# A two-layer hybrid transformer block on one Trainium2 core: 1/rms rows spread in one pass of 96 rows, modulation rows summed on four column groups, wider h tiles

## The chip, the cores and the metric

One core of a Trainium2 chip runs the whole program. TensorE multiplies matrices into PSUM, VectorE and ScalarE work on vectors, and the DMA queues are driven by SyncE. The metric is the time of one execution on the device in microseconds (us), lower is better, as the median of several runs.

## What is computed

Two layers of a diffusion trunk act on 512 latent and 256 context tokens of width 1024, all in float32. Cut to what matters here:

```python
def rms_norm(x, g):
    y = x * lax.rsqrt(jnp.mean(x * x, axis=-1, keepdims=True) + EPS)
    return y * g

mod_x = silu(c) @ w_mod + b_mod            # 6 x 1024 numbers a layer, for latents; mod_c for context
hx = rms_norm(x, norm1_g) * (1 + sc1x) + sh1x
parts = split(hx @ w_in)                   # q, k, v (and a gate) of four head groups
q = rope_2d(rms_norm(to_heads(q), qnorm_g), rows, cols)      # rms over a head of 64 or 32
out = concat(windowed, differential, retention, neighbourhood attention)
x = x + g1x * (out @ w_out)
h2 = rms_norm(x, norm2_g) * (1 + sc2x) + sh2x
x = x + g2x * (square(relu(h2 @ w_mlp1)) @ w_mlp2)
```

The context tokens go through the same weights in the first layer; in the second one only the latents are carried to the end.

## The kernel before

Activations stand transposed: features on the 128 partitions, tokens along the row, eight tiles of 128 x 768 for a width of 1024. Every large product is split into a rounded part and a rest, each of which TensorE takes in its one-pass float32 type (`F32R`), and is made of three products: `gemm` (L317, L318, L322) runs hi x hi, hi x lo and lo x hi over the feature chunks, first 512 columns, then the remaining 256 or 258. Its moving operand comes from the h tiles (`htile`, names hh, hl, oh, ol) or from the mid tiles of the MLP (mh, ml). `wload` brings weights by DMA (wr) and `split` makes wh on ScalarE (L275) and wl on VectorE (L276).

A norm is done in three steps. The mean of squares is a full float32 product with `gmean`, 32 output columns wide, on blocks of 256 tokens; block j writes the PSUM rows 32j to 32j+31 of one tile (L241 for heads, with two more products L243 where a term is added; L262 for the whole width). `rsqrt` turns the 32, 64 or 96 rows into 1/rms on ScalarE and VectorE. `finish` splits the result into a rounded part and a rest (rr, side by side along the row) and spreads each block over 128 partitions with two products (L257): one for the rounded part, one for the rest. Calls with 768 tokens have three blocks, those with 512 two, those with 256 one; all of the first layer's attention has three, the second layer's has three for keys and two for queries and head outputs.

The modulation of the first layer is computed partly on TensorE (L346, `mod_mm`, four groups of 32 PSUM rows). The remaining 14 blocks of 512 numbers, two of the first layer and all twelve of the second, are worked off by `mods_dve` beside the first layer's MLP: VectorE accumulates over 1024 features into `acc` (L396, L398), partition by partition, for both vectors c and c_ctx; then the 128 partitions have to be summed. For that `acc` is split into `az` tiles and multiplied with a two-column selector (L406, four products of 512 columns), ScalarE copies the two rows out of PSUM (L408), four small transposes (L412) turn them into columns, and `mod_add` (L340) adds the bias.

`weave` lays out the attention: a stream of input projections fills in between the attention units by hand-set cost numbers, and a scheduler orders each engine's instructions from that. Each engine then works its queue in order.

Of the kernel before, what the change touches and what calls it, by code (L numbers as in the profile page):

```python
# [12 lines left out]
OP = mybir.AluOpType  # L13
# [141 lines left out]
def body(ctx: ExitStack, tc, A):  # L155
# [18 lines left out]
    def pst():  # L174
        return pp.tile([128, 512], F32, name=nm("pt"), tag="pt", bufs=PTB)
# [18 lines left out]
    spread = cons.tile([128, 3, 128], F32R, name="spread")  # L194
    with tc.tile_pool(name="sp0", bufs=1) as sp0:
        t = sp0.tile([128, 3, 128], F32, name="spread0")
        V.memset(t, 0.0)
        for j in range(3):
            V.tensor_copy(t[32 * j:32 * j + 32, j].rearrange("p (g c) -> p g c", c=32),
                          ident[32 * j:32 * j + 32, 32 * j:32 * j + 4].unsqueeze(2).to_broadcast([32, 4, 32]))  # L200
        S.activation(spread, t, AF.Copy)
# [24 lines left out]
    sel2 = cons.tile([128, 2, 2], F32, name="sel2")  # L226
    V.memset(sel2, 0.0)
    for v in range(2):
        V.memset(sel2[:, v, v:v + 1], 1.0)
    sel2r = cons.tile([128, 2, 2], F32R, name="sel2r")  # L230
    S.activation(sel2r, sel2, AF.Copy)

    def rstd(ps, sq, n, w, rr, add=None):

        nb = n // 256
        pm = ps[-1][0][0:32 * nb, 0:256]
        for j in range(nb):
            pj = pm[32 * j:32 * j + 32]  # L240
            T.matmul(pj, lhsT=gmean[w], rhs=sq[:, 256 * j:256 * j + 256], start=True, stop=add is None)  # L241
            for i in range(0 if add is None else 2):
                T.matmul(pj[:, 128 * i:128 * i + 128], lhsT=add[:, 8 * j + 4 * i:8 * j + 4 * i + 32], rhs=ident, start=False, stop=(i == 1))  # L243
        finish(pm, ps, sq, rr, add is None)

    def finish(pm, ps, sq, rr, eps=True):

        n = pm.shape[0]
        q, e3 = sq[0:n, 0:256], sq[0:n, 256:512]
        rsqrt([(pm, 0, 256)], q, e3, 256, eps)  # L250
        rr = rr[0:n]
# [177 lines left out]
    def norm_stat(pm, y, s, l, pools=(pst, pst)):  # L429

        ps = [(f()[:, :b], a, b) for f, (a, b) in zip(pools, [(0, l)] if l < 512 else halves(l))]
        finish(pm[0:l // 8, 0:256], ps, zm(), main.tile([128, 768], F32R, name=nm("rr"), tag="zm", bufs=2))
        for p, a, b in ps:
            S.activation(y[:, s + a:s + a + b], p, AF.Copy)
        return y[:, s:s + l]
# [15 lines left out]
    def htile(p):  # L451
        return main.tile([128, 770], F32R, name=nm(p), tag="h", bufs=16)
# [13 lines left out]
    for L in range(DEPTH):  # L466
# [369 lines left out]
        def at_b(u, q, k, v):  # L836
# [4 lines left out]
            for hh in range(2):  # L841
                rows = slice(64 * hh, 64 * hh + 64)
                for n2 in range(nblk // 2):
# [25 lines left out]
                    for i in range(0, len(kts), 2):  # L869
# [7 lines left out]
                        for a in range(2):  # L877
# [6 lines left out]
            lsq = cons.tile([128, 56], F32, name=nm("lsq"), tag="lsq", bufs=1)  # L884
            V.memset(lsq, EPS)
            S.activation(lsq[:, 0:4 * nblk].rearrange("p (n h c) -> p n h c", h=2, c=2),
                         l0[:, 0:nblk].unsqueeze(3).to_broadcast([128, nblk, 2, 2]), AF.Square, scale=EPS ** 0.5)
# [208 lines left out]
        finish(ms[0:nq // 8, 0:256], ps, zm(), main.tile([128, 768], F32R, name=nm("rr"), tag="zm", bufs=2))  # L1096
# [203 lines left out]
```

## Time and profile before

| | us |
|---|---|
| median of 3 runs | 1883.28 (1882.71 to 1885.18) |
| profiled execution | 1887.48 |
| its span, first to last instruction | 1885.7 |
| busy: TensorE / its weight loads / VectorE / ScalarE | 1847.7 / 1520.6 / 1301.7 / 981.6 |

The span falls into the start (up to about 30 us), the first layer's attention (to 525), its output projection, the first layer's MLP (560 to 1095), the norm between the layers, the second layer's attention (1135 to 1505), and the output projection and MLP of the second layer (to 1880). The profile is read from the engines' busy times, then by stage, then by the rows of single instructions. A matrix product's recorded length includes its way through the pipeline, so records overlap; the distance from one start to the next tells what it occupies.

### The profile page before, as it was taken

What the parts mean: (1) busy time and instruction counts of PE and PEld (TensorE: products, weight loads), DVE (VectorE), ACT (ScalarE), POOL (GpSimd) and SP (SyncE); (2) the same over time, 40 slices, a digit from 0 to 9 for tenths busy, and PEclk for the clock granted to TensorE, in tenths of its full rate; (3) what the DMA queues carried; (4) which work ended last, traced back from release to release, by engine and by line L of the source; (5) the groups of instructions that cost most, each with busy time, mean ns of one, the idle gap of its engine ahead of it and who ended that gap; (6) DMA issues with size and microseconds to landing.
All of it is one profiled execution on the core that took longest, in us unless ns stands there. A gap on an engine that the chain in (4) does not pass through costs nothing.

```text
span 1885.7 us, 29731 instructions
## 1 busy us (share of the span) xinstructions
PE 1847.7 (98%) x10899; PEld 1520.6 (81%) x10899; DVE 1301.7 (69%) x3005; ACT 981.6 (52%) x1934; POOL 0.2 (0%) x4
## 2 busy tenths in 40 slices
PE   7998999999999999999999999999999999999999
PEld 3786777778868888888888777888677788989897
DVE  5787877788767847847847367898888664545453
ACT  4677766768563323323324356877677663434241
POOL 0000000000000000000000000000000000000000
PEclk8999999999999999999999999999999999999999
DMA  8324434432323433433422352233243233232222
GB/s 299 100 83 117 126 106 124 148 101 65 123 85 115 145 101 112 150 97 116 152 90 90 112 170 87 79 106 84 78 135 97 75 100 97 91 99 92 96 90 95
DMA packets 110418, 208.69 MB, mean 111 GB/s; under 512 B 14272, under 2 KB 20160, under 8 KB 110272
## 3 DMA queue, kind: packets, MB, share of 16 engines
q1 hardware_dynamic: 110272, 206.78, 34.9%
q8 instruction: 86, 1.41, 0.3%
q14 instruction: 60, 0.49, 0.1%
HBM read 182.09 MB, written 5.24 MB: 99 GB/s over the span
## 4 chain that ended last, share of the span: by engine, by line
PE 83%; ACT 4%; DVE 3%; DMA 1%; issue 1%; DVEq 0%; ACTq 0%
PE mm L317 22%; PE mm L318 22%; PE mm L322 22%; PE ps L701 2%; PE po L707 2%; PE po L709 2%; PE ps L854 1%; PE ps L262 1%; PE pt L873 1%; PE pt L241 1%; PE mm L346 1%; PE pt L257 1%; ACT pth L275 1%; ACT P L756 1%; PE pt L406 1%
## 5 line engine op out<-in xcount | busy, mean ns | idle before, releaser
L275 ACT ACTIVATE wh<-wr 128x512 fp32r<-128x512 f32 (+1 forms) x414 | 253.3, 614 | 592.2 <-PE mm L318 541.1
L317 PE MATMUL mm<-hh,wh 128*128 128x512 f32 (+2 forms) x1680 | 521.2, 329 | 1.0 <-ACT hh L443 0.6
L318 PE MATMUL mm<-hl,wh 128*128 128x512 f32 (+2 forms) x1680 | 518.2, 327 | 0.0
L276 DVE TENSOR_TENSOR wl<-wr,wh 128x512 fp32r<-128x512 f32 (+1 forms) x414 | 275.0, 667 | 203.3 <-ACT wh L275 133.4
L322 PE MATMUL mm<-hh,wl 128*128 128x512 f32 (+2 forms) x1680 | 362.6, 326 | 2.3 <-DVE wl L276 2.3
L317 PEld LDWEIGHTS mm<-hh,wh 128*128 128x128 f32 x1680 | 318.5, 190 | 37.1 <-issue 9.4
L318 PEld LDWEIGHTS mm<-hl,wh 128*128 128x128 f32 x1680 | 318.0, 189 | 30.3 <-issue 5.3
L322 PEld LDWEIGHTS mm<-hh,wl 128*128 128x128 f32 x1680 | 262.7, 189 | 30.5 <-issue 3.1
L317 PE MATMUL mm<-mh,wh 128*128 128x512 f32 (+1 forms) x768 | 264.4, 356 | 0.3 <-DVE mh L1120 0.3
L318 PE MATMUL mm<-ml,wh 128*128 128x512 f32 (+1 forms) x768 | 264.5, 355 | 0.0
L322 PE MATMUL mm<-mh,wl 128*128 128x512 f32 (+1 forms) x768 | 180.7, 355 | 0.0
L317 PEld LDWEIGHTS mm<-mh,wh 128*128 128x128 f32 x768 | 145.0, 189 | 23.1 <-DVE mh L1120 0.9
L318 PEld LDWEIGHTS mm<-ml,wh 128*128 128x128 f32 x768 | 145.1, 189 | 22.2 <-issue 1.6
L398 DVE SCALAR_TENSOR_TENSOR acc<-wm,silp,acc 128x512 f32<-128x512 f32 x196 | 140.8, 747 | 22.3 <-DMA wm<-in_wmod_dram 21.6
L322 PEld LDWEIGHTS mm<-mh,wl 128*128 128x128 f32 x768 | 131.2, 189 | 23.3 <-issue 3.7
L276 DVE TENSOR_TENSOR ptl<-pt,pth 128x512 fp32r<-128x512 f32 (+3 forms) x148 | 92.3, 631 | 30.4 <-ACT pth L275 28.0
L707 PE MATMUL po<-pth,vv 128*128 128x256 f32 (+2 forms) x328 | 105.8, 329 | 3.5 <-ACT pth L275 2.8
L1131 DVE SCALAR_TENSOR_TENSOR x<-mm,modc,x 128x512 f32<-128x512 f32 (+1 forms) x96 | 63.2, 658 | 61.9 <-PE mm L322 61.9
L275 ACT ACTIVATE pth<-pt 128x512 fp32r<-128x512 f32 (+3 forms) x148 | 80.0, 547 | 29.2 <-PE pt L873 17.3
L1115 DVE TENSOR_TENSOR zq<-mm,nacc 128x256 f32<-128x256 f32 (+1 forms) x128 | 61.9, 485 | 45.2 <-PE mm L322 43.1
L707 PEld LDWEIGHTS po<-pth,vv 128*128 128x128 f32 x328 | 62.1, 190 | 26.2 <-ACT pth L275 18.8
L709 PE MATMUL po<-ptl,vv 128*64 128x256 f32 (+2 forms) x256 | 77.6, 315 | 2.5 <-DVE ptl L276 2.3
(251 smaller groups left out, 2684.4 us busy)
## 6 DMA issues: line engine op xcount, KB each, us to landing
wr<-in_w_dram SPq DMA_DIRECT2D x272, 256.0 KB, 2.6
wm<-in_wmod_dram SPq DMA_DIRECT2D x112, 256.0 KB, 2.8
wr<-in_win_dram SPq DMA_DIRECT2D x96, 256.0 KB, 3.1
wr<-in_wmodh_dram SPq DMA_DIRECT2D x48, 256.0 KB, 3.3
st<-sp SPq DMA_DIRECT2D x96, 96.0 KB, 2.2
w<-in_wmod_dram SPq DMA_DIRECT2D x16, 384.0 KB, 7.0
tx<-in_dd_dram SPq DMA_DIRECT2D x8, 512.0 KB, 3.6
zm<-in_dd_dram SPq DMA_DIRECT2D x16, 256.0 KB, 3.0
```

What stands on the lines that cost most here:

```text
L241: T.matmul(pj, lhsT=gmean[w], rhs=sq[:, 256 * j:256 * j + 256], start=True, stop=add is None)
L275: S.activation(hi, src, AF.Copy)
L276: V.tensor_tensor(lo, src, hi.bitcast(F32), op=OP.subtract)
L317: T.matmul(p, lhsT=w[k][0], rhs=act[k][0][:, s:s + l], start=(k == 0), stop=False)
L318: T.matmul(p, lhsT=w[k][0], rhs=act[k][1][:, s:s + l], start=False, stop=False)
L322: T.matmul(p, lhsT=w[k][1], rhs=act[k][0][:, s:s + l], start=False, stop=(k == n - 1))
L398: V.scalar_tensor_tensor(acc[:, v], r, sil[:, k, v:v + 1], acc[:, v], op0=OP.mult, op1=OP.add)
L701: T.matmul(o, lhsT=x, rhs=y, start=(i == 0), stop=(i == 1))
L707: T.matmul(po[:, c0:c0 + l], lhsT=vv[:, hh, t], rhs=ph, start=start, stop=stop)
L709: T.matmul(po[0:64, c0:c0 + l], lhsT=vv[:, hh, t, 0:64], rhs=pl, start=False, stop=False)
L1115: V.tensor_tensor(r[:, s:s + l], p[:, :l], y2[:, s:s + l], op=OP.mult)
L1131: V.scalar_tensor_tensor(xx, p, modc[:, 40 + m, s // 512:s // 512 + 1], xx, op0=OP.mult, op1=OP.add)
```

## The change

**Spreading.** `gmean` now holds its columns twice, at 0 to 3 and at 4 to 7 of the 32. So in each group of 32 rows the means, and 1/rms, stand twice. One VectorE operation makes rr = q * isrest - hi: rows 0 to 3 become the negated rounded part, rows 4 to 7 the rest. `spread` holds -1 for the first and +1 for the second, so one product per block gives their sum. It always works on 96 rows: `rstd` and `meansq` fill all three groups, repeating blocks where there are fewer than three (`j % nb`).

**Modulation rows.** `acc` goes to TensorE unsplit, as a full float32 operand, against 32 columns of ones: four products of 256 columns, each with its own group of 32 output columns (PSUM rows 0, 32, 64, 96). ScalarE copies 128 x 256 out, two transposes of 128 x 128 follow, and one VectorE operation picks the columns and adds the bias.

**h tiles.** 784 instead of 770 columns, that is 3136 instead of 3080 bytes a partition (which the allocation rounded to 3104).

```diff
-            V.memset(t[w * g:w * g + w, w // 32 * g:w // 32 * g + w // 32], 1.0 / (w if w < 128 else D))
+            for d in (0, 4):
+                V.memset(t[w * g:w * g + w, d + w // 32 * g:d + w // 32 * g + w // 32], 1.0 / (w if w < 128 else D))
...
     def rstd(ps, sq, n, w, rr, add=None):
         nb = n // 256
-        pm = ps[-1][0][0:32 * nb, 0:256]
-        for j in range(nb):
-            pj = pm[32 * j:32 * j + 32]
-            T.matmul(pj, lhsT=gmean[w], rhs=sq[:, 256 * j:256 * j + 256], start=True, stop=add is None)
+        pm = ps[-1][0][0:96, 0:256]
+        for j in range(3):
+            pj, b = pm[32 * j:32 * j + 32], j % nb
+            T.matmul(pj, lhsT=gmean[w], rhs=sq[:, 256 * b:256 * b + 256], start=True, stop=add is None)
...
-        split(q, rr[:, 0:256], rr[:, 256:512])
-        for j in range(n // 32):
+        rr, hi = rr[0:96, 0:256], rr[0:96, 256:512]
+        S.activation(hi, q, AF.Copy)
+        V.scalar_tensor_tensor(rr, q, isrest[0:96], hi.bitcast(F32), op0=OP.mult, op1=OP.subtract)
+        for j in range(nb):
             p, s, _ = ps[j // 2]
             c = 256 * j - s
-            for i in range(2):
-                T.matmul(p[:, c:c + 256], lhsT=spread[0:n, j], rhs=rr[:, 256 * i:256 * i + 256], start=(i == 0), stop=(i == 1))
+            T.matmul(p[:, c:c + 256], lhsT=spread[0:96, j], rhs=rr, start=True, stop=True)
     def meansq(pm, sq, s, l, first, final):
-        for j in range(l // 256):
-            T.matmul(pm[32 * j:32 * j + 32, 0:256], lhsT=gmean[128], rhs=sq[:, s + 256 * j:s + 256 * j + 256], start=first, stop=final)
+        for j in range(3):
+            c = s + 256 * (j % (l // 256))
+            T.matmul(pm[32 * j:32 * j + 32, 0:256], lhsT=gmean[128], rhs=sq[:, c:c + 256], start=first, stop=final)
...
             for v in range(2):
-                parts = [main.tile([128, 768], F32R, name=nm("az"), tag="zq", bufs=ZQ)[:, 0:512] for _ in range(2)]
-                split(acc[:, v], *parts)
-                for i, a in enumerate(parts):
-                    T.matmul(p[0:2, :], lhsT=sel2r[:, v, :], rhs=a, start=(v == i == 0), stop=(v == i == 1))
-            row = zm()[0:2, 0:512]
-            S.activation(row, p[0:2, :], AF.Copy)
+                x = acc[:, v].rearrange("p (a b c) -> p b a c", a=2, b=2)
+                for b in range(2):
+                    g = 32 * (2 * v + b)
+                    T.matmul(p[g:g + 32, 0:256], lhsT=ones, rhs=x[:, b], start=True, stop=True)
+            row = zm()[:, 0:256]
+            S.activation(row, p[:, 0:256], AF.Copy)
             yield 0
             p2 = pst()
-            for j in range(4):
-                T.transpose(p2[:, 2 * j:2 * j + 2], row[:, 128 * j:128 * j + 128], ident[0:2, 0:2])
-            mod_add(L, modc, p2, slice(4 * nb, 4 * nb + 4), 4)
+            for a in range(2):
+                T.transpose(p2[:, 128 * a:128 * a + 128], row[:, 128 * a:128 * a + 128], ident)
...
-        return main.tile([128, 770], F32R, name=nm(p), tag="h", bufs=16)
+        return main.tile([128, 784], F32R, name=nm(p), tag="h", bufs=16)
```

In the code after, the lines have moved: L241 is L244, L243 is L246, L257 is L260, L262 is L266, L276 is L280, L317/L318/L322 are L321/L322/L326, L346 is L350, L396/L398 are L400/L402, L406 is L411, L412 is L417, L1112/L1115 are L1120/L1123.

How it stands in the engines' queues, at three places. TensorE, at the end of the first layer's MLP, where the norm of the 512 latents is spread (pt) between products of `w2`, before:

```order
L322 MATMUL mm_11570<-mh_10868,wl_11567 128x256
L322 MATMUL mm_11570<-mh_10950,wl_11567 128x256
L257 MATMUL pt_11496<-rr_11498,spread 128x256
L322 MATMUL mm_11570<-mh_11047,wl_11567 128x256
L322 MATMUL mm_11570<-mh_11127,wl_11567 128x256
L317 MATMUL mm_11616<-mh_10518,wh_11606 128x256
L257 MATMUL pt_11496<-rr_11498,spread 128x256 x3
L318 MATMUL mm_11616<-ml_10519,wh_11606 128x256
```

And after:

```order
L321 MATMUL mm_11444<-mh_10356,wh_11434 128x256
L322 MATMUL mm_11444<-ml_10357,wh_11434 128x256
L321 MATMUL mm_11444<-mh_10438,wh_11434 128x256
L260 MATMUL pt_11322<-rr_11324,spread 128x256 x2
L322 MATMUL mm_11444<-ml_10439,wh_11434 128x256
L321 MATMUL mm_11444<-mh_10527,wh_11434 128x256
```

Four products in two places have become two in one place.

TensorE in the first layer's MLP, a block of modulation rows between two gemms with `w1`; the line behind the gap is the transposes, one gemm later. Before:

```order
L322 MATMUL mm_6657<-hh_6398,wl_6653 128x258
L322 MATMUL mm_6657<-hh_6434,wl_6653 128x258
L406 MATMUL pt_6714<-az_6715,sel2r 2x512
L406 MATMUL pt_6714<-az_6716,sel2r 2x512
L406 MATMUL pt_6714<-az_6721,sel2r 2x512
L406 MATMUL pt_6714<-az_6722,sel2r 2x512
L317 MATMUL mm_6753<-hh_6182,wh_6743 128x512
...
L412 MATMUL pt_6803<-ident,zm_6727 128x2 x4
```

After:

```order
L326 MATMUL mm_6615<-hh_6359,wl_6611 128x258
L326 MATMUL mm_6615<-hh_6395,wl_6611 128x258
L411 MATMUL pt_6672<-acc_6491,ones 32x256 x4
L321 MATMUL mm_6703<-hh_6143,wh_6693 128x512
L322 MATMUL mm_6703<-hl_6144,wh_6693 128x512
...
L417 MATMUL pt_6753<-ident,zm_6677 128x128 x2
```

Four products of a two-row output have become four of 32-row outputs with the same operand `acc`, and four small transposes two full ones.

VectorE at the start of the next block (`acc` is the accumulator, wl the rests of weights, mm the results of gemms). Before, the splits of the old block's `acc` stand ahead of the new block's first line L396:

```order
L1115 TENSOR_TENSOR zq_6982<-mm_6924,nacc_6450 128x512
L276 TENSOR_TENSOR az_7066<-acc_6883,az_7065 128x512
L276 TENSOR_TENSOR az_7072<-acc_6883,az_7071 128x512
L276 TENSOR_TENSOR wl_7094<-wr_7091,wh_7093 128x512
L396 TENSOR_SCALAR acc_7233<-wm_7234,silp 128x512 x2
L1112 COPY b_6983<-mm_6925 128x2
L1115 TENSOR_TENSOR zq_6982<-mm_6925,nacc_6450 128x256
L276 TENSOR_TENSOR wl_7100<-wr_7097,wh_7099 128x512
```

After:

```order
L1123 TENSOR_TENSOR zq_7019<-mm_6954,nacc_6411 128x512
L280 TENSOR_TENSOR wl_7112<-wr_7109,wh_7111 128x512
L1120 COPY b_7020<-mm_6955 128x2
L1123 TENSOR_TENSOR zq_7019<-mm_6955,nacc_6411 128x256
L280 TENSOR_TENSOR wl_7118<-wr_7115,wh_7117 128x512
L400 TENSOR_SCALAR acc_7171<-wm_7172,silp 128x512 x2
L402 SCALAR_TENSOR_TENSOR acc_7171<-wm_7176,silp,acc_7171 128x512
L1128 CAST mh_7027<-zq_7019 128x768
```

The new block's first line L400 now stands behind the evacuation (L1120, L1123) of mm_6955, the gemm just ahead of that block's L411 in TensorE's queue.

## Rows read from the trace of the kernel before

**Rows 1.** Page: busy us (share of the span) and instructions of each engine.

```profile
PE 1847.7 (98%) x10899; PEld 1520.6 (81%) x10899; DVE 1301.7 (69%) x3005; ACT 981.6 (52%) x1934; POOL 0.2 (0%) x4
```

**Rows 2.** Stages: bounds, length, busy PE PEld DVE ACT POOL, granted clock, DMA.

```profile
560.00:1095.00 535.00, 534.68 (x2995) 455.62 (x2995) 347.10 (x596) 171.33 (x275) 0.00 (x0) 1.00 0.36 116
1230.00:1330.00 100.00, 98.19 (x574) 81.15 (x573) 87.61 (x241) 73.69 (x149) 0.00 (x0) 0.98 0.30 85
1330.00:1430.00 100.00, 94.48 (x453) 69.21 (x453) 84.28 (x165) 67.55 (x132) 0.00 (x0) 0.97 0.36 111
```

**Rows 3.** TensorE's waits, whole span: waiter <- releaser: us in all, times, longest.

```profile
PE ps L262 <- ACT zq L418: 9.9, 6, 7.3
PE ps L854 <- DVE sm L728: 3.8, 5, 2.6
...
PE ps L854 <- DVE of L889: 0.2, 1, 0.2
```

**Rows 4.** Largest group of L257 of 64 rows: shape, count | busy us, mean ns.

```profile
L257 PE MATMUL pt<-rr,spread 64*128 64x256 f32 x32 | 8.0, 329 | 0.0
```

**Rows 5.** Timeline of TensorE: start us, length, line, operation, count; 96-row products.

```profile
150.72 0.63 PE L257 MATMUL pt<-rr,spread 96*128 96x256 f32 x4
151.18 0.29 PE L701 MATMUL ps<-ks,qs 128*128 128x256 f32 x1
```

**Rows 6.** Timeline of TensorE: 64-row products, one alone and three together.

```profile
1102.23 0.38 PE L257 MATMUL pt<-rr,spread 64*128 64x256 f32 x1
1102.54 0.50 PE L322 MATMUL mm<-mh,wl 128*128 128x256 f32 x2
...
1170.44 0.61 PE L257 MATMUL pt<-rr,spread 64*128 64x256 f32 x3
1170.98 0.39 PE L318 MATMUL mm<-hl,wh 128*128 128x256 f32 x1
```

**Rows 7.** Timeline of TensorE: means in three row groups, and in one.

```profile
74.64 0.40 PE L318 MATMUL mm<-hl,wh 128*128 128x512 f32 x1
74.97 0.63 PE L241 MATMUL pt<-zq,gmean 128*32 128x256 f32 x6
75.53 0.50 PE L317 MATMUL mm<-hh,wh 128*128 128x512 f32 x1
75.86 0.39 PE L318 MATMUL mm<-hl,wh 128*128 128x512 f32 x1
...
1105.02 0.62 PE L262 MATMUL ps<-zq,gmean 128*32 128x256 f32 x2
1105.57 0.38 PE L322 MATMUL mm<-mh,wl 128*128 128x256 f32 x1
```

**Rows 8.** Timeline of TensorE: one block of modulation rows, both its steps.

```profile
579.74 1.10 PE L406 MATMUL pt<-az,sel2r 128*2 128x512 f32 x4
580.68 0.40 PE L317 MATMUL mm<-hh,wh 128*128 128x512 f32 x1
...
589.23 0.41 PE L412 MATMUL pt<-ident,zm 2*128 2x2 f32 x4
589.56 0.50 PE L317 MATMUL mm<-hh,wh 128*128 128x512 f32 x1
```

**Rows 9.** Timeline of TensorE: a pair of full transposes and the product behind.

```profile
379.89 0.38 PE L689 MATMUL pt<-ident,zq 128*128 128x128 f32 x2
380.03 0.48 PE L317 MATMUL mm<-hh,wh 128*128 128x512 f32 x1
```

**Rows 10.** Timeline of TensorE: first products of 24, from mid and from h tiles.

```profile
967.05 0.40 PE L317 MATMUL mm<-mh,wh 128*128 128x512 f32 x1
...
972.51 0.28 PE L317 MATMUL mm<-mh,wh 128*128 128x256 f32 x1
...
1002.22 0.40 PE L317 MATMUL mm<-hh,wh 128*128 128x512 f32 x1
...
1007.81 0.28 PE L317 MATMUL mm<-hh,wh 128*128 128x258 f32 x1
```

More of the change, by code (lines that the diff above doesn't have):

```diff
@@ L198, in body @@
         for j in range(3):
-            V.tensor_copy(t[32 * j:32 * j + 32, j].rearrange("p (g c) -> p g c", c=32),
-                          ident[32 * j:32 * j + 32, 32 * j:32 * j + 4].unsqueeze(2).to_broadcast([32, 4, 32]))
+            r = slice(32 * j, 32 * j + 32)
+            i0, i1 = [ident[r, 32 * j + d:32 * j + d + 4] for d in (0, 4)]
+            V.tensor_tensor(t[r, j].rearrange("p (g c) -> p g c", c=32), i1.unsqueeze(2).to_broadcast([32, 4, 32]),
+                            i0.unsqueeze(2).to_broadcast([32, 4, 32]), op=OP.subtract)
+            V.tensor_reduce(isrest[r], i1, axis=mybir.AxisListType.X, op=OP.add)
         S.activation(spread, t, AF.Copy)
@@ L224, in body @@
         V.tensor_copy(sel4[32 * i:32 * i + 32], ident[32 * i:32 * i + 32, 32 * i:32 * i + 2])
[L226 to L231, printed above, removed]
+    ones = cons.tile([128, 32], F32, name="ones")
+    V.memset(ones, 1.0)
     def rstd(ps, sq, n, w, rr, add=None):
         nb = n // 256
-        pm = ps[-1][0][0:32 * nb, 0:256]
-        for j in range(nb):
-            pj = pm[32 * j:32 * j + 32]
-            T.matmul(pj, lhsT=gmean[w], rhs=sq[:, 256 * j:256 * j + 256], start=True, stop=add is None)
-            for i in range(0 if add is None else 2):
-                T.matmul(pj[:, 128 * i:128 * i + 128], lhsT=add[:, 8 * j + 4 * i:8 * j + 4 * i + 32], rhs=ident, start=False, stop=(i == 1))
-        finish(pm, ps, sq, rr, add is None)
@@ L246, in finish @@
[L246 to L251, printed above, removed]
-        split(q, rr[:, 0:256], rr[:, 256:512])
-        for j in range(n // 32):
+        pm = ps[-1][0][0:96, 0:256]
+        for j in range(3):
+            pj, b = pm[32 * j:32 * j + 32], j % nb
+            T.matmul(pj, lhsT=gmean[w], rhs=sq[:, 256 * b:256 * b + 256], start=True, stop=add is None)
+            for i in range(0 if add is None else 2):
+                T.matmul(pj[:, 128 * i:128 * i + 128], lhsT=add[:, 16 * b + 8 * i:16 * b + 8 * i + 32], rhs=ident, start=False, stop=(i == 1))
@@ L254, in finish @@
+        finish(pm, ps, nb, sq, rr, add is None)
+    def finish(pm, ps, nb, sq, rr, eps=True):
+        q, e3 = sq[0:96, 0:256], sq[0:96, 256:512]
+        rsqrt([(pm, 0, 256)], q, e3, 256, eps)
+        rr, hi = rr[0:96, 0:256], rr[0:96, 256:512]
+        S.activation(hi, q, AF.Copy)
+        V.scalar_tensor_tensor(rr, q, isrest[0:96], hi.bitcast(F32), op0=OP.mult, op1=OP.subtract)
+        for j in range(nb):
             p, s, _ = ps[j // 2]
             c = 256 * j - s
-            for i in range(2):
-                T.matmul(p[:, c:c + 256], lhsT=spread[0:n, j], rhs=rr[:, 256 * i:256 * i + 256], start=(i == 0), stop=(i == 1))
+            T.matmul(p[:, c:c + 256], lhsT=spread[0:96, j], rhs=rr, start=True, stop=True)
@@ L402, in mods_dve @@
             for v in range(2):
-                parts = [main.tile([128, 768], F32R, name=nm("az"), tag="zq", bufs=ZQ)[:, 0:512] for _ in range(2)]
-                split(acc[:, v], *parts)
-                for i, a in enumerate(parts):
-                    T.matmul(p[0:2, :], lhsT=sel2r[:, v, :], rhs=a, start=(v == i == 0), stop=(v == i == 1))
-            row = zm()[0:2, 0:512]
-            S.activation(row, p[0:2, :], AF.Copy)
+                x = acc[:, v].rearrange("p (a b c) -> p b a c", a=2, b=2)
[4 more added lines that the diff above has]
+            S.activation(row, p[:, 0:256], AF.Copy)
             yield 0
             p2 = pst()
-            for j in range(4):
-                T.transpose(p2[:, 2 * j:2 * j + 2], row[:, 128 * j:128 * j + 128], ident[0:2, 0:2])
-            mod_add(L, modc, p2, slice(4 * nb, 4 * nb + 4), 4)
+            for a in range(2):
+                T.transpose(p2[:, 128 * a:128 * a + 128], row[:, 128 * a:128 * a + 128], ident)
+            V.tensor_tensor(modc[:, 4 * nb:4 * nb + 4, :].rearrange("p (a b) v -> p a b v", b=2),
+                            p2[:, 0:256].rearrange("p (a v b c) -> p a b v c", a=2, v=2, b=2)[:, :, :, :, 0],
+                            colc[:, L, 16 + 4 * nb:20 + 4 * nb].rearrange("p (a b) -> p a b", b=2).unsqueeze(3).to_broadcast([128, 2, 2, 2]), op=OP.add)
             yield 0
@@ L431, in norm_stat @@
         ps = [(f()[:, :b], a, b) for f, (a, b) in zip(pools, [(0, l)] if l < 512 else halves(l))]
-        finish(pm[0:l // 8, 0:256], ps, zm(), main.tile([128, 768], F32R, name=nm("rr"), tag="zm", bufs=2))
+        finish(pm[0:96, 0:256], ps, l // 256, zm(), main.tile([128, 768], F32R, name=nm("rr"), tag="zm", bufs=2))
         for p, a, b in ps:
@@ L883, in at_b @@
                     V.tensor_tensor(raw[rows, 256 * n2:256 * n2 + 256], po[0:64, 0:256], ev[:, 0:256], op=OP.add)
-            lsq = cons.tile([128, 56], F32, name=nm("lsq"), tag="lsq", bufs=1)
+            lsq = cons.tile([128, 72], F32, name=nm("lsq"), tag="lsq", bufs=1)
             V.memset(lsq, EPS)
-            S.activation(lsq[:, 0:4 * nblk].rearrange("p (n h c) -> p n h c", h=2, c=2),
-                         l0[:, 0:nblk].unsqueeze(3).to_broadcast([128, nblk, 2, 2]), AF.Square, scale=EPS ** 0.5)
+            for d in range(2):
+                S.activation(lsq[:, 0:8 * nblk].rearrange("p (n d h c) -> p n d h c", d=2, h=2, c=2)[:, :, d],
+                             l0[:, 0:nblk].unsqueeze(3).to_broadcast([128, nblk, 2, 2]), AF.Square, scale=EPS ** 0.5)
             for p, s, l in headnorm(raw, nq, lsq):
@@ L1095, in body @@
         ps = [(pst()[:, :l], s, l) for s, l, _ in parts]
-        finish(ms[0:nq // 8, 0:256], ps, zm(), main.tile([128, 768], F32R, name=nm("rr"), tag="zm", bufs=2))
+        finish(ms[0:96, 0:256], ps, nq // 256, zm(), main.tile([128, 768], F32R, name=nm("rr"), tag="zm", bufs=2))
         for p, s, l in ps:
```

1 line of the change is left out of this document (added).

## The prediction

> **What bounds the kernel now.** I read the busy table first: TensorE is busy 98% of the span, VectorE 69%, ScalarE 52% [rows 1]. The stages come next [rows 2]: in the first layer's MLP (560 to 1095 us) TensorE is busy 534.7 of 535 us and nothing else comes near it. In the two attention stretches shown it is busy 98 and 94 of 100 us, VectorE 88 and 84, and the granted clock is 0.98 and 0.97, so there VectorE is close behind. Last, who makes TensorE wait: the first of its 19 rows belongs to the start, the second is 3.8 us in five waits and the last 0.2 [rows 3]; without the start they come to about 20 us. So a microsecond of TensorE taken out is a microsecond of the kernel in the MLPs, and most of one in the attention.
>
> Busy time overlaps in these records, so I price a product by the distance from its start to the next one's start.
>
> **The change part by part.**
>
> *Spread products of 96 rows.* A call of `finish` with three blocks of 256 columns issues six products L257 before and three after. The program has 22 such calls. Four of them take 150.72 to 151.18, so 0.115 us each [rows 5]. Removed: 22 x 3 x 0.115 = 7.6 us.
>
> *Spread products of 64 and 32 rows.* Twelve calls have two blocks, 48 products of 64 rows (32 of them in [rows 4]); one call has one block, two products of 32 rows. These cost far more than their columns. One alone takes 0.31 us to the next start (1102.23 to 1102.54), three together 0.54 [rows 6]. The products around a narrow group also stretch: where a full one of 512 columns takes 0.233 [rows 10], the one ahead of a narrow group takes 0.33 (74.64 to 74.97) and the one behind 0.33 (75.53 to 75.86) [rows 7]. I add 0.1 ahead and 0.1 behind: 0.51 alone, 0.74 for three, 0.70 for a pair. In the order before, the 64-row products stand 13 times alone, 11 times in threes and once as a pair, and the two of 32 rows alone: 13 x 0.51 + 11 x 0.74 + 0.7 + 2 x 0.51 = 16.5 us. After there are 25 products, all of 96 rows, at 0.115: 2.9. Removed: 13.6 us. Bounds: without the stretch around them 5.4 less; nothing suggests more.
>
> *Third row group of the means.* L241 and L262 now always fill three groups of 32 rows, where calls with one or two blocks filled one or two. Three groups take 0.56 us to the next start (74.97 to 75.53), one group 0.55 (1105.02 to 1105.57) [rows 7]: a group that stands beside others is free, one that stands apart costs 0.55 + 0.2 = 0.75. So the number of separate groups decides, which the order shows: L241 (with L243) 49 before and 46 after, L262 40 and 40, and L346, which isn't changed but is moved by the scheduler, 40 and 35. Eight fewer at 0.75 are 6.0 us at most. Some of the merged ones only become a second round in a longer group, and in two calls the group with L243 grows by one L241 and two L243, so the lower bound is 0. I take 3.5.
>
> *Modulation rows.* 14 blocks, all in the first MLP. Before: four L406 from 579.74 to 580.68, 0.94 us with no stretch around them, and four L412 in 0.33 plus 0.2 around them [rows 8]: 1.47. After: four fp32 products on four column groups and two full transposes. No row has exactly this form; the nearest is L241, 0.56 + 0.2 = 0.76 with three groups [rows 7]. A pair of transposes takes 0.14 (379.89 to 380.03) and the product behind it is stretched [rows 9]; I take 0.25. Saved: 1.47 - 1.01 = 0.46, times 14 = 6.4 us. Bounds: if four groups take two rounds of 0.55, the time of one group [rows 7], 14 x 0.55 = 7.7 less, so -1.3; with transposes at 0.14, 14 x 0.11 more, 8.0.
>
> Six L241 starts in 0.56 us mean that the groups run side by side. The Trainium skill speaks against that: "TensorE: Matmul & The Clock Gate", Part 3 (Packing small matmuls), says that a weight load overlaps a running product only when their row groups differ, and these four share all rows. By that rule they would run in turn; the sum would then be 23 us smaller (below). The row disagrees: three groups in the time of one.
>
> The splits of `acc` (28 on ScalarE, 28 on VectorE) go too. They are hidden beside TensorE in that stage and earn nothing. What is new is a wait: the next block's first L400 on VectorE overwrites `acc`, which now TensorE reads, not VectorE itself; behind it stand the weight splits (L276 before, L280 after) and the evacuations. In the order, the gemm just ahead of each of the 13 L411 that have a successor is the one that VectorE evacuates just before that L400. The wait is then 0.76 us less the evacuation: nothing.
>
> `finish` itself keeps its chain: a ScalarE copy and one VectorE operation. The first product now needs the second of them, but the last one always did: 0.
>
> *h tiles.* Nothing in the instructions changes, only where tiles lie: in the built programs nearly all tiles stood 32 bytes past a multiple of 64, and h tiles alternately on it; after, all stand on it. The one sign that placement matters is that 24 products of 512 columns take 5.59 us from h tiles (1002.22 to 1007.81) but 5.46 from mid tiles (967.05 to 972.51), 5.4 ns each [rows 10]. But the mid tiles all stand off the multiple and half of the h tiles on it, and the h tiles are the slower ones: the multiple of 64 isn't what counts there. So I take 0. Bounds: if all 2256 products of 512 columns from h tiles fell to the mid tiles' time, -12 us; nothing excludes +12.
>
> *Sum.* 7.6 + 13.6 + 3.5 + 6.4 = 31.1 us of TensorE. About 21.5 of it lies in the attention stages (20 of the 22 three-block calls, ten of the twelve two-block ones, the merged groups). There VectorE is at 84 to 88% [rows 2], and I give 4 back to longer waits. Net 27. The profiled execution took 1887.5; 1860.5 on that scale. The median of the runs is 4.2 lower: **1856**.
>
> **The rivals.**
>
> *The attention gives most back.* For: VectorE at 88%, waits on it, and a granted clock at 0.97, so a wait that grows can cost a piece of half clock (3 us per 100 at 0.97). Against: waits are 2% of those stages now. If only a quarter of 21.5 arrives: 9.6 + 5.4 = 15 saved, less a piece or two of clock: 1864 to 1874, most likely 1869.
>
> *h tiles gain as well.* 1856 - 12 = 1844, 1839 to 1848. Against: half of these tiles stand on the multiple already, and they are the slower kind [rows 10].
>
> *The four column groups run in turn.* Four times the 0.55 us of one group, 2.2 + 0.2 against 0.76, 14 times: 23 us back, 1879, at the edge of what can be told from no change. Against: three groups start and are done in 0.56 us [rows 7]. The Trainium skill's rule quoted above would give this case.
>
> *Slower.* VectorE stands at the new L400 until TensorE has worked off the gemm queued ahead of L411, at least its 512-column half of 5.6 us [rows 10], and the weight splits behind come late. It decides from 31 / 13 = 2.4 us of TensorE's time per block on; at 3.5 a block it is 45 us lost: 1900. Against: the order puts the evacuation of that gemm ahead of the L400 already.
>
> *Nothing to see.* The change does what it says, but placement costs what the rest gains, 27 us or 12 ns on each of the 2256 products: 1880 to 1887.
>
> **How the numbers follow.** Forecast as summed, 1848 to 1864: 0.67. Attention gives back: 0.14. h tiles gain: 0.10. Groups in turn: 0.02. Nothing to see: 0.03. Slower: 0.04. The range 1842 to 1870 holds the first case, half of the h case and most of the second, about 0.83. Under 0.2% (3.8 us) this kernel can't be told from no change. Faster: 0.67 + 0.14 + 0.10 + 0.02 = 0.93; same 0.03; slower 0.04.
>
> **What would show it.** In the profile after: L260 as 91 products of 96 rows, 0.115 us apart, with no stretched neighbour; L411 as one group of about 0.56 us and no idle VectorE ahead of L400; separate groups of the means still 0.75; the first MLP about 6 us shorter, the second layer's attention 10 or more. I am wrong if TensorE's idle time in the attention grows by over 8 us, if L411 takes near 2 us, or if h products' distance leaves 0.233.

## The result, and the profile after

The changed kernel takes 1859.43 us (median of 4 runs, 1857.77 to 1859.82), the kernel before 1883.62 beside it: 24.2 us less, a ratio of 0.9865 (95% interval 0.9852 to 0.9877). The forecast was 1856, a gain of 27, in a range of 1842 to 1870. The profiled execution took 1859.82, and the forecast on that scale was 1860.5.

The busy table of the page of after answers to [rows 1]:

```profile
PE 1816.2 (98%) x10928; PEld 1503.1 (81%) x10928; DVE 1286.8 (69%) x2985; ACT 958.9 (52%) x1909; POOL 0.2 (0%) x4
```

TensorE is still the bound and has 31.5 us less busy time. For the stages I cut both traces at the starts of the same gemm products (the 1st, 1401st, 4601st and 5801st of 7920): start, first layer's attention, its output projection with MLP and norm, second layer's attention with its output projection, rest. The columns are bounds, length, busy PE, PEld, DVE, ACT, POOL, granted clock, DMA share, GB/s. Before:

```profile
0.00:60.42 60.42, 47.10 (x300) 26.99 (x301) 35.18 (x164) 26.75 (x50) 0.20 (x4) 0.89 0.68 246
60.42:540.15 479.73, 469.28 (x2875) 370.62 (x2873) 386.29 (x1025) 332.67 (x723) 0.00 (x0) 0.99 0.37 111
540.15:1147.08 606.93, 605.66 (x3405) 507.91 (x3405) 398.90 (x701) 215.07 (x365) 0.00 (x0) 1.00 0.37 117
1147.08:1545.93 398.85, 390.10 (x2206) 309.96 (x2205) 325.02 (x824) 288.21 (x593) 0.00 (x0) 0.99 0.32 94
1545.93:1885.70 339.77, 335.57 (x2122) 305.14 (x2120) 156.31 (x294) 118.86 (x204) 0.00 (x0) 1.00 0.29 94
```

And after:

```profile
0.00:55.38 55.38, 40.73 (x296) 23.63 (x297) 35.08 (x172) 25.98 (x48) 0.20 (x4) 0.94 0.74 269
55.38:532.77 477.39, 463.80 (x2829) 368.35 (x2828) 387.63 (x1026) 331.10 (x726) 0.00 (x0) 0.97 0.37 111
532.77:1131.28 598.51, 597.00 (x3476) 502.55 (x3475) 382.45 (x673) 196.95 (x337) 0.00 (x0) 1.00 0.37 119
1131.28:1518.77 387.49, 379.29 (x2213) 303.67 (x2212) 325.37 (x824) 286.14 (x595) 0.00 (x0) 0.99 0.33 97
1518.77:1858.01 339.24, 335.36 (x2122) 304.94 (x2120) 156.28 (x294) 118.77 (x204) 0.00 (x0) 1.00 0.29 94
```

The lengths fall by 5.0, 2.3, 8.4, 11.4 and 0.5 us. Length less busy time is TensorE's idle time: it grows from 13.3 to 14.7 in the start and from 10.4 to 13.6 in the first attention, and shrinks from 8.8 to 8.2 in the second; over the whole span it grows by 3.8 (38.0 to 41.8). The stretches of half clock (granted clock 0.5), added up over the clock record inside the span, take about 19 us of full speed in either trace (0.7 less in after), in other places. So TensorE's work at full clock fell by 27.7 + 3.8 - 0.7 = 30.8 us, where the sum said 31.1.

The first attention is the odd one. The same decomposition gives 10.6 us of work removed there, but 3.1 go back to idle time and 5.1 to half clock, and 2.3 arrive. That is one pair of profiles: after with h tiles of 770 columns, where every queue has the same order, passes on 4.9 of 11.1. In the first 60 us it is the other way round: the clock is 0.94 where it was 0.89, worth 3.4 us that no part of the change explains.

Single products in the timeline of TensorE of after (start, length, line, operation, count): a block of modulation rows, its two transposes, and spread products in a two-block and in a three-block call.

```profile
572.05 0.64 PE L411 MATMUL pt<-acc,ones 128*32 128x256 f32 x8
572.62 0.50 PE L321 MATMUL mm<-hh,wh 128*128 128x512 f32 x1
572.96 0.39 PE L322 MATMUL mm<-hl,wh 128*128 128x512 f32 x1
...
581.17 0.38 PE L417 MATMUL pt<-ident,zm 128*128 128x128 f32 x2
581.30 0.49 PE L321 MATMUL mm<-hh,wh 128*128 128x512 f32 x1
...
1145.08 0.40 PE L260 MATMUL pt<-rr,spread 96*128 96x256 f32 x2
1145.32 0.40 PE L326 MATMUL mm<-hh,wl 128*128 128x512 f32 x1
1145.56 0.39 PE L321 MATMUL mm<-hh,wh 128*128 128x512 f32 x1
...
323.54 0.62 PE L260 MATMUL ps<-rr,spread 96*128 96x256 f32 x3
324.00 0.28 PE L321 MATMUL mm<-hh,wh 128*128 128x256 f32 x1
```

Four column groups together take 0.57 us to the next start, what three took in [rows 7], and the product behind is stretched as there. The transposes take 0.13. The spread products take 0.12 each (two) and 0.15 each (three; that row is the slowest of 21 such groups, whose median is 0.12), and the gemm product behind the pair takes 0.24, so it isn't stretched; a single one of 64 rows took 0.31 in [rows 6].

### The profile page after: what moved, and what is told of

Read it like the earlier page. It is cut to its first block, busy times and chain, and to the rows that moved or that the text cites. A ratio compares the mean times of both kernels' runs of the same rounds, so it can differ in the third digit from the quotient of the medians.

```text
span 1858.0 us, 29749 instructions
## 1 busy us (share of the span) xinstructions
PE 1816.2 (98%) x10928; PEld 1503.1 (81%) x10928; DVE 1286.8 (69%) x2985; ACT 958.9 (52%) x1909; POOL 0.2 (0%) x4
## 5 line engine op out<-in xcount | busy, mean ns | idle before, releaser
L321 PE MATMUL mm<-hh,wh 128*128 128x512 f32 (+2 forms) x1680 | 522.6, 330 | 1.3 <-ACT hh L450 1.1
L322 PE MATMUL mm<-hl,wh 128*128 128x512 f32 (+2 forms) x1680 | 518.9, 327 | 0.0
L280 DVE TENSOR_TENSOR wl<-wr,wh 128x512 fp32r<-128x512 f32 (+1 forms) x414 | 275.2, 666 | 208.6 <-ACT wh L279 136.5
L326 PE MATMUL mm<-hh,wl 128*128 128x512 f32 (+2 forms) x1680 | 356.4, 325 | 1.5 <-DVE wl L280 1.5
L321 PEld LDWEIGHTS mm<-hh,wh 128*128 128x128 f32 x1680 | 319.1, 190 | 42.9 <-issue 10.1
L322 PEld LDWEIGHTS mm<-hl,wh 128*128 128x128 f32 x1680 | 319.5, 190 | 28.1 <-issue 3.9
L326 PEld LDWEIGHTS mm<-hh,wl 128*128 128x128 f32 x1680 | 261.4, 189 | 26.7 <-DVE wl L280 1.8
L321 PE MATMUL mm<-mh,wh 128*128 128x512 f32 (+1 forms) x768 | 265.0, 356 | 0.4 <-DVE mh L1128 0.3
L322 PE MATMUL mm<-ml,wh 128*128 128x512 f32 (+1 forms) x768 | 264.2, 355 | 0.0
L326 PE MATMUL mm<-mh,wl 128*128 128x512 f32 (+1 forms) x768 | 181.1, 355 | 0.0
L321 PEld LDWEIGHTS mm<-mh,wh 128*128 128x128 f32 x768 | 144.8, 189 | 24.1 <-ACT wh L279 2.5
L322 PEld LDWEIGHTS mm<-ml,wh 128*128 128x128 f32 x768 | 145.1, 189 | 22.0 <-issue 1.6
L402 DVE SCALAR_TENSOR_TENSOR acc<-wm,silp,acc 128x512 f32<-128x512 f32 x196 | 139.7, 746 | 32.1 <-DMA wm<-in_wmod_dram 31.8
L326 PEld LDWEIGHTS mm<-mh,wl 128*128 128x128 f32 x768 | 131.1, 189 | 24.1 <-issue 4.5
L714 PE MATMUL po<-pth,vv 128*128 128x256 f32 (+2 forms) x328 | 105.9, 328 | 4.2 <-ACT pth L279 3.4
L280 DVE TENSOR_TENSOR ptl<-pt,pth 128x512 fp32r<-128x512 f32 (+3 forms) x148 | 92.1, 630 | 24.9 <-ACT pth L279 22.6
L714 PEld LDWEIGHTS po<-pth,vv 128*128 128x128 f32 x328 | 62.2, 190 | 25.6 <-ACT pth L279 18.1
L1123 DVE TENSOR_TENSOR zq<-mm,nacc 128x256 f32<-128x256 f32 (+1 forms) x128 | 61.9, 484 | 26.8 <-PE mm L326 25.0
L716 PE MATMUL po<-ptl,vv 128*64 128x256 f32 (+2 forms) x256 | 77.6, 316 | 2.1 <-DVE ptl L280 1.9
```

The lines of the kernel that those rows point to most:

```text
L321: T.matmul(p, lhsT=w[k][0], rhs=act[k][0][:, s:s + l], start=(k == 0), stop=False)
L322: T.matmul(p, lhsT=w[k][0], rhs=act[k][1][:, s:s + l], start=False, stop=False)
L326: T.matmul(p, lhsT=w[k][1], rhs=act[k][0][:, s:s + l], start=False, stop=(k == n - 1))
L402: V.scalar_tensor_tensor(acc[:, v], r, sil[:, k, v:v + 1], acc[:, v], op0=OP.mult, op1=OP.add)
L714: T.matmul(po[:, c0:c0 + l], lhsT=vv[:, hh, t], rhs=ph, start=start, stop=stop)
L716: T.matmul(po[0:64, c0:c0 + l], lhsT=vv[:, hh, t, 0:64], rhs=pl, start=False, stop=False)
```

## Experiments: the parts apart

Four kernels separate the three parts of the change. The theory was that each term of the sum stands for itself and the h tiles do nothing; the rival, that placement of the h tiles carries part of the gain.

**Modulation part alone**, in the kernel before.

```diff
-                    T.matmul(p[0:2, :], lhsT=sel2r[:, v, :], rhs=a, start=(v == i == 0), stop=(v == i == 1))
+                    T.matmul(p[g:g + 32, 0:256], lhsT=ones, rhs=x[:, b], start=True, stop=True)
```

> The kernel before with the modulation part alone (unsplit acc, four column groups, two full transposes). Theory (each term of the sum stands for itself): 14 blocks of 1.47 us fall to 1.01, 6.4 to 6.6 us less, 1877 against 1883.6. Rival (the changed kernel's gain in that stage came from the wider h tiles, the modulation form earns little): 0 to 2 us less, 1882 to 1884.

Measured: 1876.04 us against 1884.54, 8.5 less; the ratio 0.9957 (0.9944 to 0.9969) allows 5.8 to 10.5. The theory holds. In its trace the stretch from the 1501st to the 4301st gemm product, which holds all 14 blocks, is 7.05 us shorter, 0.3 of it idle time.

**Spread part alone**, in the kernel before.

```diff
-        split(q, rr[:, 0:256], rr[:, 256:512])
+        S.activation(hi, q, AF.Copy)
+        V.scalar_tensor_tensor(rr, q, isrest[0:96], hi.bitcast(F32), op0=OP.mult, op1=OP.subtract)
```

> The kernel before with the spread part alone (means doubled in their columns, one product of 96 rows a block, three row groups always filled). Theory: 24 to 25 us of TensorE's work go, some 4 come back as waits and half clock in the attention, 1863 to 1865. Rival (what the whole change earned beyond the modulation came in part from the h tiles): 1868 to 1875.

Measured: 1866.49 us, 18.1 less than before (0.9903, 0.9888 to 0.9918). Between the two expectations, nearer to the theory. Added to the modulation part it makes 26.6, where the whole change makes 24 to 25: nothing is left for the h tiles to earn.

**h tiles alone**, before with 784 and after with 770 columns.

```diff
-        return main.tile([128, 770], F32R, name=nm(p), tag="h", bufs=16)
+        return main.tile([128, 784], F32R, name=nm(p), tag="h", bufs=16)
```

> The kernel before with h tiles of 784 columns and nothing else: every engine's order of instructions stays as it was, only addresses move. Theory (placement doesn't matter): 1883.6 within 1 us, and 0.233 us for a product of 512 columns from h tiles as before. Rival (placement is worth something): products from h tiles at the mid tiles' 0.2275, 12 us less, 1872; or the other way, 1895.

> The changed kernel with h tiles of 770 columns again. Theory: 1859.4 within 1.5 us. Rival (the h tiles carry part of the gain): 4 to 12 us slower, 1863 to 1871.

Measured: 1883.83 us against 1884.54 (0.9994, 0.9985 to 1.0003), and 1859.21 where after has 1859.43. The rival is out: the h tiles' width moves the time by less than can be told. It isn't quite nothing in the trace. The first of 24 products from h tiles in the kernel before with 784 columns, and the product behind them:

```profile
998.97 0.39 PE L317 MATMUL mm<-hh,wh 128*128 128x512 f32 x1
...
1004.51 0.28 PE L317 MATMUL mm<-hh,wh 128*128 128x258 f32 x1
```

5.54 us, where [rows 10] has 5.59: 2 ns each. Over the whole traces, some 1480 distances from one such product to the next at full clock, the mean falls by 0.8 ns, and by 0.8 ns between after's 770 and 784 columns too. The order of instructions is the same in each pair, so this is placement alone, and too little to see in the time.

## Experiments: what makes a spread product dear

The prediction's largest term, 13.6 us, said that products of 64 and 32 rows are dear for their shape. The rival: each product costs about the same, and halving their number is what pays. One kernel changes the shape and keeps the number, the other halves the number and keeps the shape.

**96 rows, still two products a block**, in the kernel before.

```diff
-        for j in range(nb):
-            pj = pm[32 * j:32 * j + 32]
+        for j in range(3):
+            pj, b = pm[32 * j:32 * j + 32], j % nb
```

> The kernel before with three row groups always filled, so that all spread products have 96 rows, but still two of them a block (rounded part and rest apart). Theory (the narrow products are dear for their shape): 50 narrow products that cost 16.5 us become 50 of 0.115, 5.75; 10.8 us of TensorE less; the order keeps its 143 separate groups of means, so nothing there; some 1.5 back as waits: 1874. Rival (the number of products is what counts): the number stays, 1882 to 1884.

**One product a block, only as many rows as blocks**, in the changed kernel.

```diff
-        pm = ps[-1][0][0:96, 0:256]
-        for j in range(3):
+        pm = ps[-1][0][0:32 * nb, 0:256]
+        for j in range(nb):
```

> The changed kernel with only as many row groups as there are blocks, so one product a block, of 64 rows (24) or 32 (1). In the order 22 of the 64-row ones stand in pairs. Theory: 11 pairs at 0.70 and three alone at 0.51 are 9.2 us against 2.9: 6.3 slower, 1865.7. The groups of means stay 135. Rival (the number of products counts): 1859 to 1861.

Measured: 1873.25 us (10.8 less than before, 0.9942, 0.9929 to 0.9954) and 1860.67 (0.9876, 0.9861 to 0.9891, which can't be told from after's 0.9865). The first came as the theory had it in time; but its trace has only 7.2 us less work for TensorE, and 5.8 less half clock than that of before, so part of that agreement is the clock's. The second didn't: 1.2 us instead of 6.3. The timelines of the two kernels, first the one with 96 rows, then the one with 64:

```profile
1102.08 0.35 PE L257 MATMUL pt<-rr,spread 96*128 96x256 f32 x1
1102.26 0.40 PE L323 MATMUL mm<-mh,wl 128*128 128x256 f32 x2
1102.50 0.28 PE L318 MATMUL mm<-mh,wh 128*128 128x256 f32 x1
1102.62 0.53 PE L257 MATMUL pt<-rr,spread 96*128 96x256 f32 x3
1102.99 0.28 PE L319 MATMUL mm<-ml,wh 128*128 128x256 f32 x1
```

```profile
1143.01 0.50 PE L261 MATMUL pt<-rr,spread 64*128 64x256 f32 x2
1143.43 0.50 PE L327 MATMUL mm<-hh,wl 128*128 128x512 f32 x1
1143.77 0.39 PE L322 MATMUL mm<-hh,wh 128*128 128x512 f32 x1
```

The shape's price is there in both. The single product takes 0.18 where that of 64 rows at the same place took 0.31 [rows 6], and the three behind it 0.37, where three of 64 rows took 0.54; and a pair of 64 rows takes 0.42, with the product behind it stretched to 0.34, where after has 0.24 and 0.24. But the price per call is not the price of the edit. Added up over the second attention's traces from start to start (idle time and half clock taken out), the narrow kernel's spread products and gemms take 1.6 and 2.3 us more than after's, 3.9 in all; its groups of means (L244, L246 in after) take 1.0 less, with 44 products fewer, and the remaining products 1.7 less, for which I have no cause. So the third row group isn't free as I had it: about a quarter of what the wide shape earns there goes to filling it. In the first attention nothing is narrow, and both kernels agree there.

## Experiments: what the attention does with a gain

The change passed on 2.3 of 10.6 us in the first attention. To see whether more taken from TensorE there would still arrive, I took out a larger piece: the squares are written rounded, so that the means of squares run in the one-pass type.

**All squares rounded**, with a scratch tile that this needs in the head norms.

```diff
-            T.matmul(pj, lhsT=gmean[w], rhs=sq[:, 256 * b:256 * b + 256], start=True, stop=add is None)
+            T.matmul(pm, lhsT=gmean[w][:, 64 - 32 * j:160 - 32 * j], rhs=sq[:, 256 * b:256 * b + 256], start=(j == 0), stop=(j == 2 and add is None))
...
-        finish(pm, ps, nb, sq, rr, add is None)
+        finish(pm, ps, nb, zq(), rr, add is None)
```

> The changed kernel with the squares written rounded and the means of squares taken in the one-pass type: three products of 96 output columns, weights zero but for one block of 32, that add up in the same 96 rows, where three full float32 products of 32 columns stood. A mean of squares loses the bits that the rounding of its squares takes. Theory (a separate float32 group of 32 columns costs 0.76 for its shape and type, a full-width one-pass product 0.118): 86 groups go from 0.76 to 3 x 0.118 = 0.35, 35 us of TensorE less; the attention, where half of them stand, gives some 8 back: 1832. Rival (VectorE holds the attention, and 40 of the groups lie there): 1843 to 1850. Nothing gained: 1858.

Measured: 1857.46 us, 2 less than after. The trace has 30.6 us less work for TensorE than after's, and 16 us more idle time and 13 more half clock. All of the idle time lies in the two attentions; of the half clock, 6.8 us lie in the second attention and 5.1 in the start. I took that for an attention at VectorE's edge, and split it up.

**Only outside the attention; only in the head norms; only the scratch tile.** The last is the second hunk above, in the changed kernel, with its arithmetic.

> The changed kernel with rounded squares and one-pass means (three products of 96 columns) only for the norms over the whole width, that is outside the attention; the head norms stay in full float32. Theory (outside the attention TensorE alone sets the time, so what is taken from it arrives whole; it was the attention that gave everything back in the run with all squares rounded): 4.3 us in the first layer's output projection, 6.4 around its MLP, some 3 in the second layer's output projection, as that run's trace shows: 14 less, 1845. Rival (one-pass means bring waits or half clock of their own wherever they stand): 1855 to 1859.

> The changed kernel with rounded squares and one-pass means only for the head norms, that is in the attention, and, as that needs, a scratch tile of its own for 1/rms from the zq buffers. Theory (the attention is at VectorE's and ScalarE's edge and gives back more than it gets): some 15 us of TensorE less, and 1857.5 + 14 = 1871 in time. Rival (the attention passes the gain on, the norms outside are what cost): 1845.

> The changed kernel with nothing but that scratch tile: the head norms make 1/rms in a tile of their own from the zq buffers and not in the tile of the squares; arithmetic as in the changed kernel. Theory (the loss in the attention is TensorE waiting for VectorE and ScalarE, not for buffers): 1859.4 within 2 us. Rival (one more tile from these buffers holds the attention up): the 12 us of the run with rounded heads, 1868 to 1872.

Measured: 1848.74, 1863.76 and 1883.73 us. The first goes the theory's way (10.7 of 14). The second lies between its two expectations, 4.3 slower than after. The third throws the theory over: the scratch tile alone, with no work added, costs 24.3 us, as much as the whole change earned, and against it the rounded heads earn 20.0, with 18.8 us less work in the trace. The attention does pass gains on; what it doesn't bear is that tile. Its two attention stages, and TensorE's longest waits in the whole span (waiter, releaser: us, times, longest):

```profile
55.31:542.88 487.57, 466.57 (x2830) 369.20 (x2828) 386.12 (x1026) 328.18 (x726) 0.00 (x0) 0.98 0.36 109
1141.10:1542.55 401.45, 384.33 (x2213) 304.69 (x2212) 325.79 (x824) 286.12 (x595) 0.00 (x0) 0.98 0.32 93
```

```profile
PE ps L266 <- ACT zq L425: 11.0, 7, 7.8
PE ps L244 <- ACT zm L828: 7.2, 6, 1.8
PE po L714 <- ACT pth L279: 6.0, 14, 0.7
```

VectorE and ScalarE do the same work as in after, in a longer time, so neither became the bound. TensorE idles 21.0 and 17.1 us in these stages, where after has 13.6 and 8.2. The second row, which after's list doesn't have, is the head norms' means waiting for their squares. One of the six places, in the timeline of after and then of the kernel with the scratch tile:

```profile
236.08 1.07 PE L350 MATMUL mm<-wr,silp 128*32 128x256 f32 x16
237.08 0.50 PE L321 MATMUL mm<-hh,wh 128*128 128x512 f32 x1
237.42 0.39 PE L322 MATMUL mm<-hl,wh 128*128 128x512 f32 x1
237.65 0.40 PE L321 MATMUL mm<-hh,wh 128*128 128x512 f32 x1
237.98 0.40 PE L244 MATMUL ps<-zm,gmean 128*32 128x256 f32 x1
```

```profile
236.47 1.06 PE L350 MATMUL mm<-wr,silp 128*32 128x256 f32 x14
238.34 0.40 PE L244 MATMUL ps<-zm,gmean 128*32 128x256 f32 x1 [0.80 <-ACT zm L828]
```

In after three gemm products stand ahead of the means and fill the time until the squares are there; with the scratch tile they stand behind, and TensorE waits. Over the eight head norms the number of gemm products ahead of the means is smaller by 3, 18, 3, -7, 23, 38, 37 and 23. So the queue was laid out in another order, with the same instructions: some 2200 of TensorE's 10928 places hold another product than in after. The kernels with rounded squares and this tile have the same counts of gemm products ahead of the means, but for one at the last norm.

**The same with six zq buffers**, to tell a lack of buffers from the order; **and rounded everywhere, but in place**: 1/rms is made in the tile that held rr, and rr goes into that of the squares, so that no tile is added.

```diff
-ZQ = 5
+ZQ = 6
```

```diff
-        finish(pm, ps, nb, zq(), rr, add is None)
+        finish(pm, ps, nb, rr.bitcast(F32), sq, add is None)
```

> The run with the scratch tile alone, but with six instead of five zq buffers (and h tiles of 770 columns, which made no difference, to have the room). Theory (the 24 us were engines waiting for one of five buffers): with a sixth 1859 to 1863. Rival (not the buffers but a chain that grew longer, or the order in which the engines' queues were laid): 1878 to 1885.

> The changed kernel with all squares rounded and all means in one pass, and without the extra scratch tile: 1/rms is made in the tile that held rr, and rr goes into the tile of the squares, so that the number of tiles stays. Theory (the extra tile cost the 24 us, and rounding the heads' squares earned 20 against the run with the tile alone): 1848.7 - 20.0 = 1829. Rival (the tile of the squares, now held until the spread products have read it, holds the attention up as the extra tile did): 1848 to 1857.

Measured: 1885.96 us (1.0004 of before, 0.9995 to 1.0013): the sixth buffer changes nothing, and TensorE's queue is laid out as with five at all eight head norms (115 places differ in all). A lack of buffers is out as a cause. The waits at L828 are 7.2 of the 16 us of idle time more; that the order explains the other waits, and the half clock that follows, wasn't tried, and why one more tile changes the order stays open.

In place: 1827.49 us, 57 less than before (0.9694, 0.9680 to 0.9707) and 32 less than after, as the sum of the parts had it. The means of the whole width there, and the first attention's stage:

```profile
1053.11 0.61 PE L273 MATMUL ps<-zqr,gmeanr 128*96 128x256 f32 x3
1053.56 0.62 PE L333 MATMUL mm<-mh,wl 128*128 128x512 f32 x2
```

```profile
59.34:521.16 461.82, 447.92 (x2771) 364.16 (x2770) 385.37 (x1022) 329.22 (x723) 0.00 (x0) 0.99 0.39 115
```

Three one-pass products take 0.45 us where a float32 group takes 0.56 and stretches its neighbours [rows 7]. In the first attention TensorE idles 13.9 us, about as in after, and the stage is 15.6 us shorter: 10.8 us of work less and 5.1 of half clock. In the second 11.6 us of work go and 8.2 arrive, since idle time grows by 5.1 there, while half clock falls by 1.7. So most of the gain arrives, not all of it.

## Why the prediction was right, and where its size was off

**The bound and the sum.** Right: TensorE's work fell by 30.8 us where 31.1 were summed. The pair of profiles followed with 27.7 us, the medians with 24.2.

**Modulation rows.** Right: L411 takes 0.57 and a stretched neighbour (0.76 predicted with it), the transposes 0.13, and the part alone earned 5.8 to 10.5 us for 6.4. That four column groups run in turn is refuted by the row of L411. The Trainium skill ("TensorE: Matmul & The Clock Gate", Part 3, Packing small matmuls), by which products that share their rows would not overlap their weight loads, doesn't describe these: in after the eight weight loads of the row at 572.05 us take 0.16 us together, beside its products, the first of which starts with them. That the products would run in turn was my inference from that rule, which speaks of weight loads alone.

**The wait at the new L400.** It isn't there: VectorE sits idle ahead of L400 once, 2.2 us, and for a DMA.

**Spread products and means.** Together about right (24.7 summed; 25.9 us less work in the trace of that part alone, 3.7 of it in the start), apart less so. The 13.6 us for narrow products are too much by what the run with 96 rows and two products showed, 7.2 us of work for 10.8; and of the 3.5 for merged groups, 2.0 came: 1.1 from the means and 1.5 from L350 in the first attention, while the second pays 0.6 more for the filled third group. Part of what made up for it in the sum is the start, where TensorE's work is 3.0 us less (40.3 to 37.3) and the sum has one call in it, 0.3 us. The traces of this case scatter from 36.3 to 42.5 there, so that the total came out within 0.3 us is in part luck. The rest I can't name row by row.

**h tiles.** Right: nothing that can be told in the time.

**What the attention gives back.** This is the term that was mis-sized. I had 21.5 us of work less in the two attentions and put 4 of it into waits. In the traces 19.7 us of work go there and 6.0 come back: idle time grows by 2.6, and half clock by 3.4 (5.1 more in the first attention, 1.7 less in the second). The half clock behind the waits I had left to a rival. From 140 to 265 us the kernels with one spread product a block differ from those with two. The kernel before, and the one with 96 rows and two products:

```profile
140.00:265.00 125.00, 117.99 (x730) 89.91 (x729) 100.39 (x316) 85.32 (x198) 0.00 (x0) 0.95 0.41 116
```

```profile
140.00:265.00 125.00, 117.71 (x733) 89.53 (x730) 100.67 (x314) 85.70 (x199) 0.00 (x0) 0.96 0.42 116
```

After, and the kernel with the spread part alone:

```profile
140.00:265.00 125.00, 115.86 (x698) 88.17 (x697) 100.47 (x310) 82.50 (x190) 0.00 (x0) 0.90 0.40 112
```

```profile
140.00:265.00 125.00, 115.88 (x713) 87.99 (x712) 101.32 (x311) 84.20 (x195) 0.00 (x0) 0.93 0.41 116
```

The kernel with wider h tiles alone and that with the modulation part alone have 0.96 here, after with 770 columns 0.92, the narrow kernel with one product a block 0.93. So in these four traces with one product TensorE is 2 us less busy, and half clock costs 8.5 to 11.9 us of full speed over these 125, where it costs 5.1 to 6.8 in the four with two products. Two places differ in all eight: near 202 us the four with one product lose 1.7 us to half clock and the others nothing, and near 247 us they lose 5.1 where the others lose 3.4. The kernel rounded in place, which has one product a block too, but less work in its means, has 0.95 over these 125 us and loses nothing near 202. The first of the two places, in after: TensorE's busy time from 194 to 203 us and then the clock, and four rows of its timeline in that stretch.

```profile
194.00:203.00 9.00, 7.12 (x49) 4.53 (x47) 7.42 (x25) 5.50 (x12) 0.00 (x0) 1.00 0.36 117
203.00:207.20 4.20, 4.20 (x12) 3.28 (x13) 4.17 (x10) 2.62 (x6) 0.00 (x0) 0.60 0.37 122
```

```profile
200.05 0.38 PE L861 MATMUL ps<-st,st 128*128 128x256 f32 x1 [0.24 <-DVE sm L735]
200.72 0.38 PE L861 MATMUL ps<-st,st 128*128 128x256 f32 x1 [0.29 <-DVE sm L735]
201.47 0.38 PE L714 MATMUL po<-pth,vv 128*128 128x256 f32 x1 [0.37 <-ACT pth L279]
202.20 0.33 PE L716 MATMUL po<-ptl,vv 128*64 128x256 f32 x1 [0.34 <-DVE ptl L280]
```

The same four products in the kernel before, where L854, L707 and L709 are these lines:

```profile
206.60 0.38 PE L854 MATMUL ps<-st,st 128*128 128x256 f32 x1
207.44 0.36 PE L707 MATMUL po<-pth,vv 128*128 128x256 f32 x1
207.78 0.31 PE L709 MATMUL po<-ptl,vv 128*64 128x256 f32 x1
210.96 0.28 PE L854 MATMUL ps<-st,st 128*128 128x256 f32 x1
```

None of them waits there, and the clock stays at 1.00 from 188 to 252 us. The attention's products L861, L714 and L716 now come to the front of TensorE's queue before VectorE and ScalarE have made what they read: gaps of 0.2 to 0.4 us, and half clock behind them. The same four waits, each within 6 ns, stand in the other three traces with one product and in none of the other three with two; the kernel rounded in place has the first of them alone, and no half clock behind it. So the half clock goes with the waits in all nine traces; no run took the waits away and left all else.

**From the profile to the median.** The profiled execution of before stood 4 us above its median, and I took the same for after. That step failed: after's stands 0.4 above its own. Before's profile carried more half clock than most; the kernel with the same order and other addresses had a profiled execution of 1881.5 us and a mean clock of 0.992, not 0.990. So the pair of profiles, 27.7 us apart, overstates the gain of 24.2 by 3.5, and the forecast of 1856 missed 1859.4 by as much. Every run on record has its mean clock beside it: half clock costs the kernel before 15.5 us of full speed in the mean of 54 runs (19.4 in its profile), and after 18.6 in the mean of 8 runs with 784 or 770 columns. These 3 us are close to the 3.4 that the two places above cost in the attention, and the pair of profiles hides them, since before's profile happened to lose as much elsewhere. That the forecast on the profile's scale, 1860.5, came within 0.7 us of 1859.82 is luck.

## What to carry to other kernels

Where one engine is busy nearly all the time, price a change by start-to-start distances in its own queue, and add the stretched neighbours: that sum held to 1% here, in part by luck, while single terms erred by some 3 us. Count the half clock that follows new idle time as part of what a stage gives back, and compare several profiles, or the mean clocks of all runs, before trusting a difference of a few us between two. And when a small edit costs far more than its work, look first at whether the queue was laid out in another order: one scratch tile cost as much here as the whole change earned.

## What the runs showed of the hardware

Four float32 products of 32 output columns on four column groups take no longer than three or one (0.57, 0.56, 0.55 us). A float32 product of 32 columns is dear for its shape and type: three one-pass products of 96 columns do the same sums of squares that are written rounded, and replacing 0.76 us groups by them was worth another 32 us. And moving h tiles by some bytes changes a 512-column product by 1 to 2 ns.
